# A hybrid decoder layer on one core: the S5 projection of the last four tiles and the first mixer's units of tile 4 placed earlier, four low parts moved to VectorE

## The chip, the cores and the metric

The kernel runs on one core of one Trainium2 chip. The metric is the device time of one execution in microseconds (us); less is better. The names of the engines in the rows are: PE is TensorE (matmuls), PEld its weight loads, DVE is VectorE, ACT is ScalarE, POOL is GpSimd, SP is SyncE, which here only issues transfers.

## What is computed

One decoder layer on x (1024 rows of 1024), float32. The input projection feeds three mixers: A is sliding-window attention with sinks, B is an S5 state-space layer, C is sparse attention with three branches. The three outputs are normalised each by itself, set side by side, and projected together. A feed-forward part follows.

```python
h = rms_norm(x, norm1_g[l]) * (1 + sc1) + sh1
aq, ak, av, su, cq, ck, cv, cg = jnp.split(h @ w_in[l], offsets, axis=-1)
o_a = swa_sink_mixer(aq, ak, av, a_q_gain[l], a_k_gain[l], a_sinks[l])   # 384 columns
o_b = s5_mixer(su, ...)                                                  # 256 columns
o_c = nsa_mixer(cq, ck, cv, cg, ...)                                     # 384 columns
mix = jnp.concatenate([rms_norm(o_a, g_a), rms_norm(o_b, g_b), rms_norm(o_c, g_c)], axis=-1)
x = x + ga1 * (mix @ w_out[l])
h = rms_norm(x, norm2_g[l]) * (1 + sc2) + sh2
x = x + ga2 * (jnp.square(jax.nn.relu(h @ w_ff1[l])) @ w_ff2[l])
```

## The kernel before

**Tiles and parts.** The 1024 rows are eight tiles (0 to 7) of 128 rows. A float32 product is made of three matmuls (`mm3`): both operands are split into a high part (`copy_hi`, a copy on ScalarE to the type fp32r) and a low part (`split_lo`, the subtraction of the high part, on VectorE or GpSimd), and high by high, high by low and low by high are added up in PSUM. The output projection of one tile has eight row blocks of `w_out` ("f"): 0 to 2 belong to mixer A, 3 and 4 to mixer B (S5), 5 to 7 to mixer C, and two halves of 512 columns. So mixer B's share of one tile is 2 halves x 2 blocks x 3 = 12 matmuls of 128x512.

**Stages.** First comes the input projection with the mixers' constants. Mixer A's units of tiles 0 to 3 run beside it (`a_phase`). Then `c_phase` runs mixer C's units of tiles 0 to 3, and beside it `early_ab` projects mixers A and B of tiles 0 to 3 and then loads the blocks 5 to 7. After each of these tiles `tile_end` normalises mixer C's output, projects it, adds the residual (`residual`), and forms the second norm and its transposed high and low parts (`norm2_steps`). With tile 4 the mixed stretch begins: the mixers' units of tiles 4 to 7 (A and C) are laid out in time T one after another, and `feed_forward` gives PE the feed-forward products of the first half (tiles 0 to 3) in between; it may start when tile 3's second norm is done ("N2 3"). When all units are done, `late_proj` loads the blocks of `w_out` again and projects tiles 4 to 7, mixer A's share first, then B's, then C's, adds the residual and forms the second norm; feed-forward products of the first half stand in between. The rest is the feed-forward part of the second half.

**What sets the order.** The program is written by generators and by steps put at planned times (`put`, `at`, `spawn`); `run_plan` records the calls in the order of the planned times, and `arrange` then lists them once more: each engine takes, of the recorded calls that are ready by its own costs, the first in recorded order. The result is a fixed order per engine, in which each engine issues its instructions one after another. SBUF pages have a tag and a number of slots (`SLOTS`: 38 of tag "b"), PSUM banks are given in rotation by `take`. All instructions are issued from one line (L2191), so the rows below are told apart by tile names and shapes: pa and pb are PSUM banks, b and u are pages, k holds keys, wide holds the unit matrix with which PE transposes.

**What the change touches.** `add_y` (line 1516) adds a projected half to the tile's page `y`; the first contribution is written with a factor per row, mixer B's has none (r is None). `early_ab` (1771) ends with "WO". `late_proj` (1806) goes through the groups of blocks:

```python
late, tiles, groups = {}, range(4, NT), ((0, 1, 2), (3, 4), (5, 6, 7), ())
...
if i == 1:
    late[n] = load_b(n)
    continue
```

`c_phase` (1864) lays out the units. At tile 4 the first unit of mixer A gets a stretch of its own, in which PSUM banks are dealt out anew (`mix_banks`), and `feed_forward` follows:

```python
if n == 4 and not kv and m == "a":
    s0, T = T, T + dur
    put(s0 - 3.5, mix_banks)
    spawn(s0 + X_T, feed_forward(), "N2 3")
    soft_end = T - C_GAP
```

`load_ff` (1905) loads a block of feed-forward weights and makes its high part on ScalarE and its low part on GpSimd (`split_lo(G, ...)`).

Of the kernel before, what the change touches and what calls it, by code (L numbers as in the profile page):

```python
# [9 lines left out]
F32 = mybir.dt.float32  # L10
# [3 lines left out]
ALU = mybir.AluOpType  # L14
# [6 lines left out]
NT = 8  # L21
# [289 lines left out]
def trunk(ctx: ExitStack, tc: tile.TileContext, I, out):  # L311
# [76 lines left out]
    def put(t, what):  # L388
        made_steps[0] += 1
        heapq.heappush(heap, (t, made_steps[0], what))  # L390
# [1125 lines left out]
    def add_y(n, c, o, r):  # L1516
        if n not in y:
            y[n] = page(1024)
            fresh[n] = set()
        d = y[n][:, c]  # L1520
        if c.start not in fresh[n]:
            fresh[n].add(c.start)
            ts(d, o, r, ALU.mult)
        elif r is None:
            tt(d, o, d, ALU.add)
        else:
            stt(d, o, r, d, ALU.mult, ALU.add)
# [204 lines left out]

    oA_d = dr.tile([NT, 128, 384], F32, name="oA_d")
    oC_d = dr.tile([4, 128, 384], F32, name="oC_d")

    def a_phase():

# [33 lines left out]
    def early_ab():  # L1771

        for f in range(5):
            load_wo(f)
            yield P_WO
        for n in range(NT // 2):
            while f"a {n}" not in done or "s5" not in done:
                yield 1.0
            o = load_o(oA_d[n])
            mb = load_b(n)  # L1780
            st = []
            steps = finish_steps(st, n * 2, lambda: o, 64, "b") + proj_steps(n, [0, 1, 2], st) + proj_steps(n, [3, 4], mb)
            for f in steps:
                f()
                yield P_TILE / len(steps)
        for f in range(5, 8):
            load_wo(f)
            yield P_WO
        load_row(2)
        done.add("WO")  # L1790

    def tile_end(n):

# [11 lines left out]

    def late_proj():

        late, tiles, groups = {}, range(4, NT), ((0, 1, 2), (3, 4), (5, 6, 7), ())
        for f in groups[0]:
            load_wo(f)  # L1810
            yield L_PACE
        for i, fs in enumerate(groups[:3]):
            for n in tiles:
                yield L_PACE
                if i == 1:
                    late[n] = load_b(n)
                    continue
                o, late[n] = load_o(oC_d[n - 4] if i else oA_d[n]), []
                for step in finish_steps(late[n], n * 2 + (16 if i else 0), lambda: o, 64 + fs[0]):
                    step()  # L1820
                    yield L_PACE
            for n in tiles:
                for dh in range(2):
                    c, o = slice(dh * 512, dh * 512 + 512), take("f2")
                    for j, f in enumerate(fs):
                        mm3(o, *late[n][0](j), WO[f][0][:, c], WO[f][1][:, c], j == 0, j == len(fs) - 1)
                    add_y(n, c, o, late[n][1])
                    yield L_PACE * len(fs)
                if 0 < n - 3 <= len(groups[i + 1]):
                    load_wo(groups[i + 1][n - 4])  # L1830
# [33 lines left out]
    def c_phase():  # L1864
# [10 lines left out]
        for n in range(NT):  # L1875
            units = [("a", kv, 0) for kv in range(2)] if n >= 4 else []
            units += [("c", kv, br) for kv in range(2) for br in (1, 2)]
            for m, kv, br in units:
                if m == "a":
                    dur = X_A  # L1880
                else:
                    np_ = (n + 1 if br == 1 else min(n + 1, 5)) + ((br == 2) == (n == NT - 1))
                    dur = np_ * (C_PART if n < 4 else X_PART) + C_FIX
                s0 = max(soft_end, T - dur * C_LEAD - C_GAP)
                soft_end = T - C_GAP
                if n == 4 and not kv and m == "a":
                    s0, T = T, T + dur
                    put(s0 - 3.5, mix_banks)
                    spawn(s0 + X_T, feed_forward(), "N2 3")
                    soft_end = T - C_GAP  # L1890
                unit_steps(m, n, kv, br, T, s0, soft_end, dur, Q)
                T += dur
                if n >= 4 and kv and br != 1:
# [11 lines left out]
    def load_ff(unit):  # L1905
# [2 lines left out]
        raw, hi, lo = page(1024), page(1024), page(1024)  # L1908
        nc.sync.dma_start(out=raw, in_=I["ff1"][i] if kind == 1 else I["ff2"][i, dh])
        copy_hi(hi, raw)  # L1910
        split_lo(G, lo, raw, hi)
        w_of[unit] = hi, lo

    def ff_act(o):
# [341 lines left out]
```

## Time and profile before

| | us |
|---|---|
| median of three executions | 1365.98 |
| lowest, highest | 1362.07, 1370.18 |
| the profiled execution | 1368.67 |
| its span, first to last instruction | 1367.0 |

The span lies 1.7 us under the time of the same execution. Busy times of the profile say how long an engine had an instruction; the ends of matmuls are modelled, so PE's busy time is an upper measure. PEclk is the granted clock of TensorE as a share of 2.4 GHz. "Idle before" names what ended the wait of an engine.

### The profile page before, as it was taken

Reading aid. Unit: us, or ns where it says so; the run is one execution under the profiler, and the core shown is the slowest. Engines: PE = TensorE matmul, PEld = TensorE weight load, DVE = VectorE, ACT = ScalarE, POOL = GpSimd, SP = SyncE. Lnnn points to the kernel's source line nnn. Section 1 sums busy time; section 2 is a strip of 40 time slices with the busy share of each in tenths; the row PEclk is TensorE's granted clock in tenths of the full one; section 3 lists DMA queues with packets and bytes.
Section 4 is the critical chain, followed back from the end, with each engine's and each line's share of the span. In section 5 each row is a group of like instructions: output and inputs, shape, how many; then the busy total and the mean of one; then the engine's idle time right before and its main releaser. Section 6 shows DMA issues by size and latency. Waiting matters only on the chain.

```text
span 1367.0 us, 19734 instructions
## 1 busy us (share of the span) xinstructions
PE 1306.1 (96%) x6862; PEld 1115.3 (82%) x6862; DVE 954.8 (70%) x1979; ACT 749.3 (55%) x1657; POOL 639.1 (47%) x604
## 2 busy tenths in 40 slices
PE   5998998998999869999999999999999999999998
PEld 4898998997787558888888888888787888888886
DVE  7868977787788545465565576463558887788896
ACT  6445367567666775565565565542354445544450
POOL 3477734034567365455465465575553233122230
PEclk9999999999899789999999999999999999999999
DMA  9445436223122222212222343244464432323221
GB/s 364 177 141 170 153 117 214 95 72 116 39 76 108 89 89 69 74 64 68 95 80 62 119 144 120 75 143 146 153 223 162 155 123 78 107 94 108 78 93 62
DMA packets 59570, 161.03 MB, mean 118 GB/s; under 512 B 6447, under 2 KB 22349, under 8 KB 59469
## 3 DMA queue, kind: packets, MB, share of 16 engines
q1 hardware_dynamic: 51661, 145.86, 32.3%
q10 hardware_dynamic: 7808, 13.91, 2.7%
q8 instruction: 54, 0.88, 0.3%
q14 instruction: 47, 0.39, 0.1%
HBM read 140.59 MB, written 19.14 MB: 117 GB/s over the span
## 4 chain that ended last, share of the span: by engine, by line
PE 76%; DVE 7%; ACT 3%; issue 2%; POOL 1%; DMA 1%; ACTq 0%; DVEq 0%; SPq 0%; POOLq 0%
PE pb L2191 41%; PE pa L2191 35%; DVE b L2191 4%; ACT b L2191 2%; DVE pb L2191 1%; ACT u L2191 1%; POOL b L2191 1%; DMA mixB_d<-b 1%; DVE k L2191 1%; DVE small L2191 0%; DVE u L2191 0%; DVE s L2191 0%; DMA b<-in_ada_dram 0%; ACT s L2191 0%; ACT k L2191 0%
## 5 line engine op out<-in xcount | busy, mean ns | idle before, releaser
L2191 PE MATMUL pb<-b,b 128*128 128x512 f32 (+2 forms) x2478 | 590.2, 385 | 1.4 <-DVE b L2191 1.3
L2191 PEld LDWEIGHTS pb<-b,b 128*128 128x128 f32 (+1 forms) x2478 | 446.0, 190 | 85.7 <-DVE b L2191 2.8
L2191 POOL TENSOR_TENSOR b<-b,b 128x1024 fp32r<-128x1024 f32 (+6 forms) x140 | 322.7, 2312 | 293.2 <-ACT b L2191 188.0
L2191 PE MATMUL pa<-b,b 128*128 128x512 f32 (+2 forms) x1830 | 364.3, 349 | 9.5 <-ACT b L2191 4.4
L2191 PEld LDWEIGHTS pa<-b,b 128*128 128x128 f32 (+1 forms) x1830 | 291.7, 195 | 49.8 <-ACT b L2191 5.3
L2191 ACT ACTIVATE b<-b 128x1024 fp32r<-128x1024 f32 (+4 forms) x266 | 242.0, 927 | 100.8 <-DMA b<-in_ff_dram 42.6
L2191 DVE TENSOR_TENSOR b<-b,b 128x1024 fp32r<-128x1024 f32 (+4 forms) x181 | 200.2, 1136 | 21.8 <-ACT b L2191 12.1
L2191 PE MATMUL pa<-u,b 128*128 128x384 f32 (+2 forms) x836 | 202.0, 364 | 7.4 <-DVE small L2191 2.0
L2191 PEld LDWEIGHTS pa<-u,b 128*128 128x128 f32 x836 | 148.3, 206 | 16.2 <-ACT u L2191 4.6
L2191 DVE TENSOR_TENSOR b<-pa,b 128x512 f32<-128x512 f32 (+2 forms) x168 | 107.6, 650 | 65.3 <-PE pa L2191 61.8
L2191 ACT ACTIVATE u<-pa 128x384 fp32r<-128x384 f32 (+4 forms) x205 | 97.1, 478 | 84.3 <-PE pa L2191 83.3
L2191 DVE TENSOR_TENSOR u<-pa,u 128x384 fp32r<-128x384 f32 (+1 forms) x173 | 94.9, 553 | 55.7 <-ACT u L2191 55.2
L2191 DVE TENSOR_TENSOR b<-pb,b 128x512 f32<-128x512 f32 (+2 forms) x120 | 76.2, 647 | 60.1 <-PE pb L2191 55.2
L2191 POOL TENSOR_SCALAR b<-b,small 128x64 f32<-128x64 f32 (+8 forms) x118 | 75.2, 648 | 68.9 <-DVE small L2191 55.8
L2191 PE MATMUL pa<-wide,b 128*128 128x128 f32 (+1 forms) x443 | 81.7, 296 | 24.8 <-DVE b L2191 19.1
L2191 POOL TENSOR_SCALAR u<-u,small 128x256 f32<-128x256 f32 (+3 forms) x90 | 55.1, 623 | 100.0 <-DVE small L2191 78.4
L2191 PEld LDWEIGHTS pa<-wide,b 128*128 128x128 f32 (+1 forms) x443 | 58.4, 149 | 43.5 <-DVE b L2191 21.2
L2191 POOL TENSOR_TENSOR b<-r,b 128x512 fp32r<-128x512 f32 x37 | 51.2, 1383 | 80.6 <-ACT b L2191 80.1
L2191 ACT ACTIVATE b<-pb 128x512 f32<-128x512 f32 (+3 forms) x60 | 29.1, 509 | 87.0 <-PE pb L2191 72.4
L2191 ACT ACTIVATE u<-pb,small 128x256 f32<-128x256 f32 (+6 forms) x126 | 60.2, 485 | 28.7 <-DVE small L2191 28.0
L2191 ACT ACTIVATE b<-pb,small 128x64 f32<-128x64 f32 (+4 forms) x130 | 62.5, 493 | 20.4 <-DVE small L2191 15.6
L2191 PE MATMUL pb<-k,u 128*128 128x320 f32 (+10 forms) x300 | 70.0, 344 | 2.3 <-ACT b L2191 2.1
(145 smaller groups left out, 1446.2 us busy)
## 6 DMA issues: line engine op xcount, KB each, us to landing
b<-in_ff_dram SPq DMA_DIRECT2D x128, 512.0 KB, 3.6
b<-in_ada_dram SPq DMA_DIRECT2D x48, 512.0 KB, 6.0
b<-in_x_dram SPq DMA_DIRECT2D x16, 512.0 KB, 7.1
b<-in_wo_dram SPq DMA_DIRECT2D x16, 512.0 KB, 4.3
r<-in_w_in_dram SPq DMA_DIRECT2D x16, 256.0 KB, 2.6
b<-in_cw_dram SPq DMA_DIRECT2D x8, 512.0 KB, 5.4
x_d<-b ACTq DMA_DIRECT2D x8, 512.0 KB, 3.2
out_dram<-b SPq DMA_DIRECT2D x16, 256.0 KB, 2.2
```

What stands on the lines that cost most here:

```text
L2191: method(*args, **kw)
```

## The change

It has three parts. Mixer B's share of the output projection of tiles 4 to 7 is made at the end of `early_ab`: four times `load_b`, 12 matmuls, two copies from PSUM to a page `y`, and a store of the page to a new buffer `yB_d` in DRAM; `late_proj` loads these pages back, no longer loads blocks 3 and 4 again, and adds only A's and C's share. The two units of mixer A of tile 4 are planned like those of tiles 0 to 3 (a shorter duration, a lead before the last unit of tile 3 ends), and the banks are dealt out anew at the first unit of mixer C of tile 4. The low parts of the first four feed-forward blocks go to VectorE.

```diff
@@ add_y
         if c.start not in fresh[n]:
             fresh[n].add(c.start)
-            ts(d, o, r, ALU.mult)
+            if r is None:
+                V.tensor_copy(out=d, in_=o)
+            else:
+                ts(d, o, r, ALU.mult)
@@ trunk
     oC_d = dr.tile([4, 128, 384], F32, name="oC_d")
+    yB_d = dr.tile([4, 128, 1024], F32, name="yB_d")
@@ early_ab
         load_row(2)
         done.add("WO")
+        for n in range(NT // 2, NT):
+            steps = proj_steps(n, [3, 4], load_b(n))
+            for f in steps:
+                f()
+                yield 6.0 / len(steps)
+            nc.scalar.dma_start(out=yB_d[n - 4], in_=y.pop(n))
@@ late_proj
-        late, tiles, groups = {}, range(4, NT), ((0, 1, 2), (3, 4), (5, 6, 7), ())
+        late, tiles, groups = {}, range(4, NT), ((0, 1, 2), (5, 6, 7), ())
...
-        for i, fs in enumerate(groups[:3]):
+        for i, fs in enumerate(groups[:2]):
             for n in tiles:
                 yield L_PACE
-                if i == 1:
-                    late[n] = load_b(n)
-                    continue
+                if not i:
+                    y[n] = page(1024)
+                    nc.sync.dma_start(out=y[n], in_=yB_d[n - 4])
@@ c_phase
                 if m == "a":
-                    dur = X_A
+                    dur = X_A if n > 4 else A_DUR
...
                 if n == 4 and not kv and m == "a":
-                    s0, T = T, T + dur
-                    put(s0 - 3.5, mix_banks)
-                    spawn(s0 + X_T, feed_forward(), "N2 3")
-                    soft_end = T - C_GAP
+                    s0 = max(soft_end, T - A_LEAD - A_GAP)
+                    spawn(T + 12.0, feed_forward(), "N2 3")
+                if n == 4 and not kv and m == "c" and br == 1:
+                    put(s0 + 0.0, mix_banks)
@@ load_ff
-        split_lo(G, lo, raw, hi)
+        split_lo(V if not half and kind == 1 and i < 4 else G, lo, raw, hi)
```

Since `arrange` lists everything anew, the order changes on all engines from the end of tile 2 on. Three places follow. In the change the issuing line is L2201.

On PE, between the output projection of tile 3 (its last matmul reads b_687) and the first feed-forward product (out pb_69, the last row). wide,b_693 are the transposes of tile 3's normed rows, wide,u_691 those of a unit of mixer A of tile 4. Before:

```order
L2191 MATMUL pa_65<-b_629,b_687 128x512
L2191 MATMUL pb_67<-b_395,u_689 128x256 x4
L2191 MATMUL pb_68<-b_395,u_689 128x256 x2
L2191 MATMUL pa_64<-wide,b_693 128x128
L2191 MATMUL pa_65<-wide,b_693 128x128
L2191 MATMUL pa_64<-wide,b_693 128x128
L2191 MATMUL pa_65<-wide,b_693 128x128
L2191 MATMUL pa_64<-wide,u_691 128x128 x3
L2191 MATMUL pa_65<-wide,q_692 128x128 x3
L2191 MATMUL pb_69<-b_652,b_700 128x512
```

In the change the transposes of tile 3's normed rows read b_712 (last row); ahead of them, behind the projection of tile 3, stand now the last half of tile 7's S5 projection (its last matmul is the first row), products of mixer A's unit of tile 4 with its values (pa_66) and scores of mixer C of tile 4 (k_444):

```order
L2201 MATMUL pa_64<-b_504,u_705 128x512
L2201 MATMUL pa_66<-u_710,b_358 128x384 x2
L2201 MATMUL pb_67<-k_444,u_702 128x352 x2
L2201 MATMUL pb_68<-k_444,u_702 128x352 x2
L2201 MATMUL pa_64<-wide,u_708 128x128 x3
L2201 MATMUL pa_66<-u_715,b_357 128x384
L2201 MATMUL pb_68<-k_444,u_702 128x352 x2
L2201 MATMUL pa_64<-wide,u_708 128x128 x3
L2201 MATMUL pa_66<-u_715,b_357 128x384
L2201 MATMUL pb_67<-k_444,u_702 128x352 x2
L2201 MATMUL pa_66<-u_717,b_358 128x384 x2
L2201 MATMUL pa_65<-wide,b_712 128x128
```

Before, only six score matmuls of mixer A (b_395) stood there.

On ACT, the end of mixer C's unit of tile 3 up to the high part of its normalised output, which the projection of tile 3 reads (b_687). Before:

```order
L2191 ACTIVATE u_683<-pa_64 128x384
L2191 ACTIVATE u_684<-pa_65,small 128x384
L2191 ACTIVATE s_686<-pa_66 64x384
L2191 ACTIVATE s_688<-s_645 128x384
L2191 ACTIVATE small<-small 128x1 x2
L2191 ACTIVATE b_703<-b_702 128x1024
L2191 ACTIVATE b_687<-s_645 128x384
```

In the change (there the high part is b_700, s_699 is the end of the unit, u_708 are exponentials of the second unit of mixer A of tile 4, yB_d the store of tile 6's page):

```order
L2201 DMA yB_d<-b_692 128x1024
L2201 ACTIVATE s_699<-pa_66 64x384
L2201 ACTIVATE u_702<-pa_63,small 128x384
L2201 ACTIVATE u_708,small<-pb_67,small 128x256
L2201 ACTIVATE s_701<-s_649 128x384
L2201 ACTIVATE u_708,small<-pb_67,small 128x256
L2201 ACTIVATE u_708,small<-pb_68,small 128x256
L2201 ACTIVATE small<-small 128x1 x2
L2201 ACTIVATE b_700<-s_649 128x384
```

Exponentials of tile 4 and a store stand now where a feed-forward block's high part (b_703) stood.

On SP's queue, the loads around the blocks 5 to 7 of `w_out` in `late_proj`. Before (the three last rows are these blocks):

```order
L2191 DMA u_1204<-oC_d 128x384
L2191 DMA b_1189<-in_ff_dram 128x1024
L2191 DMA u_1207<-oC_d 128x384
L2191 DMA u_1213<-oC_d 128x384
L2191 DMA b_1192<-in_wo_dram 128x1024
L2191 DMA b_1195<-in_wo_dram 128x1024
L2191 DMA b_1198<-in_wo_dram 128x1024
```

In the change (b_1159 is block 2, b_1178 and b_1181 are blocks 5 and 6):

```order
L2201 DMA u_1195<-oC_d 128x384
L2201 DMA b_1159<-in_wo_dram 128x1024
L2201 DMA b_1162<-yB_d 128x1024
L2201 DMA b_1166<-yB_d 128x1024
L2201 DMA b_1170<-yB_d 128x1024
L2201 DMA b_1174<-yB_d 128x1024
L2201 DMA u_1198<-oC_d 128x384
L2201 DMA b_1178<-in_wo_dram 128x1024
L2201 DMA b_1181<-in_wo_dram 128x1024
```

Four loads of stored pages stand ahead of the blocks 5 to 7.

## Rows read from the trace of the kernel before

**Rows 1.** The page: span, and busy times by engine.
```profile
span 1367.0 us, 19734 instructions
PE 1306.1 (96%) x6862; PEld 1115.3 (82%) x6862; DVE 954.8 (70%) x1979; ACT 749.3 (55%) x1657; POOL 639.1 (47%) x604
```

**Rows 2.** Busy times by stretch: length, each engine's us (x instructions), PEclk, DMA share, GB/s.
```profile
405.00:432.00 27.00, 25.75 (x147) 21.39 (x145) 21.31 (x72) 17.59 (x51) 18.84 (x19) 1.00 0.34 113
432.00:444.00 12.00, 11.19 (x58) 8.72 (x58) 11.53 (x39) 10.34 (x34) 11.33 (x13) 1.00 0.37 132
444.00:452.00 8.00, 5.96 (x24) 3.09 (x22) 5.15 (x13) 7.97 (x24) 4.81 (x6) 0.88 0.39 134
452.00:460.00 8.00, 6.68 (x25) 5.10 (x25) 4.36 (x10) 6.62 (x17) 0.01 (x1) 0.50 0.19 66
460.00:472.00 12.00, 9.11 (x49) 6.30 (x47) 7.32 (x17) 8.34 (x18) 3.92 (x4) 0.93 0.06 16
480.00:489.00 9.00, 0.00 (x0) 0.00 (x0) 3.25 (x10) 5.18 (x13) 7.20 (x8) 0.73 0.34 136
505.00:900.00 395.00, 394.71 (x2003) 329.78 (x2002) 233.48 (x623) 232.70 (x556) 218.06 (x168) 1.00 0.28 90
```

**Rows 3.** Who waited for whom, PE: us in total, times, longest us.
```profile
PE pa L2191 <- DVE b L2191: 21.4, 9, 9.5
```

**Rows 4.** Timeline of PE from tile 3's output projection on: start, us, what.
```profile
472.18 6.80 PE L2191 MATMUL pa<-b,b 128*128 128x512 f32 x18 [0.54 <-ACT b L2191]
...
489.21 0.69 PE L2191 MATMUL pa<-wide,b 128*128 128x128 f32 x2 [9.52 <-DVE b L2191]
...
492.52 1.20 PE L2191 MATMUL pb<-b,b 128*128 128x512 f32 x2
```

**Rows 5.** The chain of waits in that gap: start, us, engine.
```profile
483.81 2.52 POOL b L2191
...
486.87 0.19 POOL small L2191
```

**Rows 6.** The chain in the late feed-forward part, then the timeline of PE at 515.
```profile
1030.13 27.20 PE pb L2191 x120
...
515.38 0.49 PE L2191 MATMUL pa<-wide,u 128*128 128x128 f32 x3
515.62 0.60 PE L2191 MATMUL pa<-u,b 128*128 128x384 f32 x2
516.07 2.90 PE L2191 MATMUL pb<-b,b 128*128 128x512 f32 x12
```

**Rows 7.** Instructions by form of ACT and DVE: count, busy us, mean ns, idle before.
```profile
L2191 ACT ACTIVATE u<-pb,small 128x256 f32<-128x256 f32 x6 | 2.8, 470 | 0.2 <-DVE small L2191 0.2
L2191 ACT ACTIVATE u<-s 128x256 fp32r<-128x256 f32 x3 | 1.2, 405 | 0.0
L2191 ACT ACTIVATE b<-b 128x1024 fp32r<-128x1024 f32 x11 | 11.5, 1056 | 0.0
...
L2191 DVE COPY b<-pa 128x512 f32<-128x512 f32 x4 | 2.8, 691 | 2.5 <-PE pa L2191 2.5
L2191 DVE CUSTOM_DVE_ANT_1 pb<-pb,u,small 128x256 f32<-128x256 f32 x6 | 2.7, 489 | 0.0
```

**Rows 8.** Timeline in the late projection: a POOL subtraction and two equal ones of DVE.
```profile
912.05 2.40 POOL L2191 TENSOR_TENSOR b<-b,b 128x1024 fp32r<-128x1024 f32 x1
...
912.11 2.62 DVE L2191 TENSOR_TENSOR u<-s,u 128x256 fp32r<-128x256 f32 x1
...
915.25 0.45 DVE L2191 TENSOR_TENSOR u<-s,u 128x256 fp32r<-128x256 f32 x1
```

**Rows 9.** The first late product of PE, SP's loads of blocks 5 to 7; landing (page).
```profile
908.99 2.34 PE L2191 MATMUL pa<-b,u 128*128 128x512 f32 x9
...
925.31 5.89 SPq L2191 DMA_DIRECT2D b<-in_wo_dram  x3
...
b<-in_wo_dram SPq DMA_DIRECT2D x16, 512.0 KB, 4.3
```

## The prediction

> **What bounds the kernel now.** I read the page's busy times first: PE works for 1306.1 of 1367.0 us, no other engine for more than 70% [rows 1]. So time can only be gained where PE idles, or by giving it less to do where it doesn't. The stretches tell the two apart: from 505 to 900 PE is busy for 394.71 of 395.00 us, while between 444 and 472 it has 5.96, 6.68 and 9.11 of 8, 8 and 12 us, and between 480 and 489 nothing at all [rows 2]. The list of who waited for whom names the largest wait there: PE waits 9.5 us for a page "b" of DVE [rows 3]. On PE's timeline it lies between the projection of tile 3, which ends at 472.18 + 6.80 = 478.98, and the transposes of tile 3's normed rows at 489.21; the first feed-forward product comes at 492.52, 13.5 us after the projection [rows 4]. The chain of waits shows a POOL low part of 2.52 us at 483.81, ahead of the small POOL instruction of the norm at 486.87 [rows 5]. So one transition of some 50 us is loose; what follows it is tight.
>
> The sum is made against the profiled execution, 1368.67 us (span 1367.0), which lies 2.7 above the median of 1365.98; that much is taken off at the end. A measurement here can tell about 0.5%, 6.8 us, from no change.
>
> **The change part by part.** PE's products are the same ones at other places, so each term is work moved out of a tight stretch, or into a loose one.
>
> (a) *48 products leave the tight late part.* Four tiles times 12 products of 128x512. In the tight part such a product takes 27.20/120 = 0.227 us [rows 6]: 48 x 0.227 = **-10.9**. The bounds are equal to it within 0.1, as nothing idles there.
>
> (b) *Tile 4's units have run partly before the first feed-forward product.* By PE's order this is 10 transposes, 8 products 128x384 with the values and 16 score products. The timeline gives 0.24 us for three transposes (515.38 to 515.62), so 0.08 each, and 0.45 for two products with values (515.62 to 516.07), so 0.225 each [rows 6]; a score product is put at 0.19, by its width against the 384 columns. 0.8 + 1.8 + 3.0 = **-5.6**; they leave a part in which PE is full.
>
> (c) *The transition gets longer.* The first of the eight groups of six S5 products lands between 405 and 432, where PE has 25.75 of 27 us: 6 x 0.227 = 1.4 on the path. The other seven, and tile 4's units, fall into 444 to 472. PE has 28 - 21.75 = 6.25 us free there, and its half clock besides. But ACT gets six exponentials (0.470), four copies (0.405) and some nine more of that size, less two copies of a feed-forward block (1.056), about 2.8 + 1.6 + 4.0 - 2.1 = 6.3 us; DVE gets seven copies from PSUM (0.691) and eleven masks or subtractions (0.489), 4.8 + 5.4 = 10.2 us, short readouts not counted [rows 7]. In 444 to 472 ACT is busy for 22.93 of 28 us, DVE for 16.83 [rows 2]. Nothing shows that this dependent work can be packed to 100%. I take the density of the stretch just before, 432 to 444, in which ACT has 10.34 of 12 (0.862), DVE 11.53 (0.961), PE 11.19 (0.93) [rows 2]. ACT then needs (22.93 + 6.3)/0.862 = 33.9 us, 5.9 more than the 28; DVE (16.83 + 10.2)/0.961 = 28.1, 0.1 more; PE (21.75 + 9.5 of seven groups - 4.0 of clock)/0.93 = 29.3, 1.3 more. ACT decides: 1.4 + 5.9 = **+7.3**. Ends: 1.4 if all of it fits between, 1.4 + 6.3 + 10.2 = 17.9 if every added instruction of both engines is in the chain.
>
> (d) *The clock.* The granted clock is 0.88 from 444, when PE idles a quarter of the time, 0.50 (1.2 GHz) from 452 to 460, 0.93 after [rows 2]. Tile 3's 18 products take 6.80 us [rows 4], though 18 x 0.227 = 4.1 at full clock. With PE filled before it, I expect most of the 2.7 back: **-2.0**, ends 0 and -2.7.
>
> (e) *The norm of tile 3.* On DVE there now stand between the projection's last addition and the norm's scaling also a copy (0.69), two masks (2 x 0.489), two subtractions of an attention unit (2 x 0.45) and a low part of 128x1024, put at four times the 0.45 of a 128x256 one [rows 7, 8]: 0.7 + 1.0 + 0.9 + 1.8 = 4.4. DVE issues in order, so all that stands behind them waits. Against this goes the POOL low part of 2.52 ahead of the norm's small instruction [rows 5]. **+1.9**; ends -2.5 and +4.4. The 9 us of idle PE are filled by tile 4's units, which is term (b); the gap doesn't vanish, it holds work.
>
> (f) *The late projection's loads.* Two loads of `w_out` (and their high and low parts) and eight DVE additions go; four of stored pages come, ahead of the blocks 5 to 7 on SP's queue, and the four stores on ACT's queue, of which ACT only issues the start. Before, 44.4 us lie between the first product of mixer A (908.99) and the first of mixer C (953.40); in PE's new order 112 products, 112 x 0.227 = 25.4 us. SP issues block 5 at 925.31, 16.3 us after the first product, and two more 2.9 apart; a load lands in 4.3 [rows 9], then come ACT's copy, 1.056 [rows 7], and the low part, 2.40 [rows 8], 7.8 in all. At the old offset block 5 is there at 24.1, in time for 25.4; block 7 at 16.3 + 5.9 + 7.8 = 30.0, needed six products (1.4) later than 25.4, so 3.2 too late. The pages come free earlier too, as mixer B's part is gone, so I take half: **+1.6**. Ends: 0, and 7.8 + 2 x 2.9 = 13.6 if all is exposed.
>
> (g) *Low parts to VectorE.* What stays of them on the path is in (e); one POOL product then has no such neighbour ahead of it. That more is lost by both engines working at once is a rival below.
>
> Sum: -10.9 - 5.6 + 7.3 - 2.0 + 1.9 + 1.6 = -7.7, so 1368.67 - 7.7 = 1361.0 for the profiled execution and **1358.3** for the median.
>
> **The rivals.** *R1, no room in the transition.* The added ACT and DVE work is chained (exponentials, sums, scaling, transposes, copies alternate between the engines), and (c) is 17.9 rather than 7.3: -7.7 + 10.6 = +2.9, 1368.9. For it: around 452 PE, DVE and ACT all have holes at once, a sign of a chain, not of a full engine. Against: the new work belongs to other units than the chain, so it can go into the holes. Chance 0.18.
>
> *R2, all of it fits.* (c) costs 1.4, (d) gives 2.7, (e) gives 2.5, (f) is 0: -10.9 - 5.6 + 1.4 - 2.7 - 2.5 = -20.3, 1345.7. For it: 5.1 us of ACT and 11.2 of DVE idle in 444 to 472 against 6.3 and 10.2 added. Chance 0.19.
>
> *R3, the late weights come too late (slower).* If the stored pages ahead of them on SP's queue, or pages not yet free, hold back block 5 until all 13.6 us of load, copy and low part stand exposed, and the clock falls after that hole as it does at 452, where 8 us run at 0.50 (4.0 of work lost): -7.7 + 13.6 - 1.6 + 4.0 = +8.3, 1374.3. It begins to cost when block 5 is issued later than 25.4 - 7.8 = 17.6 us after the first late product. For it: SP issues in order, and the old offset is 16.3, only 1.3 away. Against: products of the feed-forward part stand ready in the pages and the order mixes them in. Chance 0.10.
>
> *R4, DVE and POOL in each other's way.* At 912 a DVE subtraction of 128x256 takes 2.62 us while a POOL one of 2.40 runs, an equal one 0.45 when none does [rows 8]: 2.2 lost. If three of the four moved low parts, or the norm's additions beside POOL's masks, meet that, 3 x 2.2 = 6.6: -1.1, 1364.9. Against: of wide two-operand POOL work only the factor on tile 3's rows remains at that place. Chance 0.08. The Trainium skill, "SBUF — State Buffer", section "Who interferes with whom", speaks against moving work to VectorE for this reason: the pair of ports that VectorE and GpSimd share is an exclusive lock, and an instruction of one that needs it holds up the other fully. By that rule, the trace agrees: 2.62 against 0.45.
>
> That the change doesn't do what it says is excluded by the order of PE, ACT and SP, in which the moved instructions stand.
>
> **How the numbers follow.** The forecast's own case has 0.45, with 1353 to 1363 as its range; two thirds of it lie under 1365.98 - 6.8 = 1359.2. Faster by over 0.5%: 0.30 + R2's 0.19 = 0.49. Within 0.5%: 0.15 of the forecast, 0.15 of R1 and 0.07 of R4 = 0.37. Slower: R3's 0.10, 0.03 of R1, 0.01 of R4 = 0.14. The range 1346 to 1371 takes in R1, nearly all of R2 and R4; outside lie R3 and the tails of R1 and R2, under 0.2.
>
> **What would show it.** Right: between 444 and 480 the granted clock stays near 1 and PE is fuller; tile 3's 18 products take about 4.1; the wait on DVE's page shrinks below 3 us with tile 4's products inside the gap; the first feed-forward product comes near 492.5 + 7.3 - 2.0 + 1.9 = 499.7; the first late product 5.6 us of work nearer to it than before, and mixer C's follow 25 to 29 us after mixer A's. (c) is wrong if the first feed-forward product comes before 494 (R2) or after 508 (R1); (f) if PE waits over 4 us for a page of `w_out` in the late projection (R3); (g) if the moved low parts take over 3 us on DVE (R4). The forecast as a whole is wrong if 505 to 900 is no longer full on PE, since (a) and (b) rest on that.

## The result, and the profile after

| | before | change |
|---|---|---|
| median of four executions each, us | 1368.08 | 1349.93 |
| lowest, highest | 1362.07, 1370.21 | 1347.43, 1350.46 |
| the profiled execution, us (span) | 1368.67 (1367.0) | 1350.46 (1348.7) |

The ratio is 0.9873, 95% interval 0.9844 to 0.9903: 18.2 us less, and the whole interval lies under 0.995, where the prediction begins to call a change faster. Two later series of the change against the kernel before gave 0.9861 [0.9842, 0.988] and 0.9896 [0.987, 0.9922]. The forecast of 1358.3 had the direction; the time lies inside its range of 1346 to 1371, but the gain was put at 7.7 us, and the time is under the 1353 to 1363 of the forecast's own case.

The page of the change (answers to [rows 1]); PE has the same 6862 products and is busy 10.9 us less, 1295.2 for 1306.1:

```profile
span 1348.7 us, 19750 instructions
PE 1295.2 (96%) x6862; PEld 1101.7 (82%) x6862; DVE 955.1 (71%) x1983; ACT 747.5 (55%) x1655; POOL 636.2 (47%) x598
```

Where the 18 us went is not seen by setting equal times side by side, since the change runs ahead early. PE's order is the same in both kernels for its first 2470 products, so the profiles are cut here at two events that both have: product 2400, the first of five transposes of width 128, and the first feed-forward product. On PE's timeline (start, us, what), product 2400 of before, then of the change:

```profile
401.14 0.71 PE L2191 MATMUL pa<-wide,b 128*128 128x128 f32 x5
```

```profile
393.81 0.71 PE L2201 MATMUL pa<-wide,b 128*128 128x128 f32 x5
```

And the busy times by stretch (length, us of each engine with its instructions in the order PE, PEld, DVE, ACT, POOL; granted clock; DMA share; GB/s), cut at these events. Before:

```profile
0.00:401.14 401.14, 366.94 (x2400) 341.34 (x2401) 310.29 (x754) 240.42 (x625) 194.15 (x286) 0.94 0.43 145
401.14:492.52 91.38, 72.73 (x355) 55.86 (x353) 59.90 (x170) 63.83 (x177) 55.44 (x57) 0.86 0.30 101
492.52:1367.00 874.48, 866.45 (x4111) 718.08 (x4109) 584.59 (x1057) 445.10 (x856) 389.55 (x262) 1.00 0.33 107
```

The change:

```profile
0.00:393.81 393.81, 356.75 (x2401) 330.67 (x2401) 308.14 (x754) 240.62 (x625) 193.97 (x286) 0.98 0.44 148
393.81:489.12 95.31, 86.17 (x437) 65.56 (x435) 75.22 (x215) 71.10 (x203) 51.15 (x58) 0.95 0.39 131
489.12:1348.70 859.58, 852.23 (x4029) 705.48 (x4027) 571.69 (x1017) 435.75 (x827) 391.12 (x255) 0.99 0.33 109
```

Three things are to be seen. The first stretch, in which no instruction of PE, DVE, ACT or POOL was moved, is 7.3 us shorter, at a mean granted clock of 0.98 instead of 0.94. The transition holds 82 more products and is only 3.9 us longer; PE is busy for 90% of it instead of 80%, and its clock is 0.95 instead of 0.86. The late stretch holds these 82 products less and is 14.9 us shorter. 14.9 - 3.9 = 11.0 us come from the moved work in this pair, 7.3 from the part in common.

Inside the transition of the change, PE's timeline:

```profile
471.47 0.63 PE L2201 MATMUL pa<-b,b 128*128 128x512 f32 x2
471.93 0.33 PE L2201 MATMUL pa<-u,b 128*128 128x384 f32 x1
472.33 3.94 PE L2201 MATMUL pa<-b,b 128*128 128x512 f32 x16
...
485.90 0.69 PE L2201 MATMUL pa<-wide,b 128*128 128x128 f32 x2 [1.04 <-DVE b L2201]
...
489.12 0.78 PE L2201 MATMUL pb<-b,b 128*128 128x512 f32 x1
```

Tile 3's 18 products (2 + 16) now take 476.27 - 471.47 = 4.80 us where [rows 4] had 6.80, the wait of 9.52 on DVE's page is 1.04, and from the end of the projection to the first feed-forward product it is 489.12 - 476.27 = 12.85 us, against 13.54. So the way to tile 3's projection is what grew: 471.47 - 393.81 = 77.66 us, against 472.18 - 401.14 = 71.04.

DVE and POOL in that place, on their timelines:

```profile
477.87 0.69 DVE L2201 COPY b<-pa 128x512 f32<-128x512 f32 x1 [0.69 <-PE pa L2201]
...
480.08 1.21 DVE L2201 TENSOR_TENSOR b<-b,b 128x1024 f32<-128x1024 f32 x1
...
481.75 1.21 DVE L2201 TENSOR_TENSOR b<-b,b 128x1024 fp32r<-128x1024 f32 x1
...
485.09 0.75 DVE L2201 TENSOR_SCALAR b<-b,small 128x1024 f32<-128x1024 f32 x1
```

```profile
477.56 2.39 POOL L2201 TENSOR_TENSOR b<-b,b 128x1024 f32<-128x1024 f32 x1
...
482.93 0.19 POOL L2201 TENSOR_SCALAR small<-small 128x1 f32<-128x1 f32 x1 [1.45 <-ACT b L2201]
```

The moved low part takes 1.21 us on DVE (481.75), behind the residual's sum (480.08) and while ACT makes the squares, so the norm's small instruction on POOL starts at 482.93, when ACT is done; before, a low part of 2.52 us stood ahead of it [rows 5].

### The profile page after: what moved, and what is told of

Same layout as the page of the kernel before. It is cut to its first block, busy times and chain, and to the rows that moved or that the text cites. A ratio compares the mean times of both kernels' runs of the same rounds, so it can differ in the third digit from the quotient of the medians.

```text
span 1348.7 us, 19750 instructions
## 1 busy us (share of the span) xinstructions
PE 1295.2 (96%) x6862; PEld 1101.7 (82%) x6862; DVE 955.1 (71%) x1983; ACT 747.5 (55%) x1655; POOL 636.2 (47%) x598
## 4 chain that ended last, share of the span: by engine, by line
PE 71%; DVE 9%; ACT 4%; DMA 3%; issue 2%; POOL 1%; ACTq 0%; SPq 0%; DVEq 0%; POOLq 0%
PE pb L2201 40%; PE pa L2201 32%; DVE b L2201 6%; ACT b L2201 2%; ACT u L2201 1%; DVE u L2201 1%; POOL b L2201 1%; DMA b<-in_ada_dram 1%; DVE pb L2201 1%; DMA mixB_d<-b 1%; DMA r<-in_w_in_dram 1%; DVE small L2201 0%; DVE k L2201 0%; DMA oC_d<-s 0%; ACT s L2201 0%
## 5 line engine op out<-in xcount | busy, mean ns | idle before, releaser
L2201 PE MATMUL pb<-b,b 128*128 128x512 f32 (+2 forms) x2466 | 586.8, 385 | 2.1 <-DVE b L2201 1.4
L2201 PEld LDWEIGHTS pb<-b,b 128*128 128x128 f32 (+1 forms) x2466 | 443.6, 190 | 87.5 <-DVE b L2201 3.3
L2201 POOL TENSOR_TENSOR b<-b,b 128x1024 fp32r<-128x1024 f32 (+6 forms) x134 | 315.9, 2365 | 266.5 <-ACT b L2201 186.7
L2201 PE MATMUL pa<-b,b 128*128 128x512 f32 (+2 forms) x1842 | 361.6, 345 | 8.7 <-ACT b L2201 4.2
L2201 PEld LDWEIGHTS pa<-b,b 128*128 128x128 f32 (+1 forms) x1842 | 289.1, 191 | 49.0 <-ACT b L2201 4.6
L2201 ACT ACTIVATE b<-b 128x1024 fp32r<-128x1024 f32 (+4 forms) x264 | 240.0, 925 | 110.3 <-DMA b<-in_ff_dram 32.4
L2201 DVE TENSOR_TENSOR b<-b,b 128x1024 fp32r<-128x1024 f32 (+4 forms) x185 | 202.2, 1124 | 16.5 <-ACT b L2201 7.4
L2201 PE MATMUL pa<-u,b 128*128 128x384 f32 (+2 forms) x836 | 197.8, 356 | 7.4 <-DVE small L2201 2.0
L2201 DVE TENSOR_TENSOR b<-pa,b 128x512 f32<-128x512 f32 (+2 forms) x165 | 105.4, 649 | 75.4 <-PE pa L2201 71.8
L2201 PEld LDWEIGHTS pa<-u,b 128*128 128x128 f32 x836 | 143.4, 200 | 17.5 <-ACT u L2201 4.8
L2201 ACT ACTIVATE u<-pa 128x384 fp32r<-128x384 f32 (+4 forms) x205 | 96.6, 478 | 84.3 <-PE pa L2201 81.0
L2201 DVE TENSOR_TENSOR u<-pa,u 128x384 fp32r<-128x384 f32 (+1 forms) x173 | 94.2, 552 | 48.0 <-ACT u L2201 47.4
L2201 POOL TENSOR_SCALAR u<-u,small 128x256 f32<-128x256 f32 (+3 forms) x90 | 59.0, 666 | 125.8 <-DVE small L2201 69.2
L2201 POOL TENSOR_SCALAR b<-b,small 128x64 f32<-128x64 f32 (+8 forms) x118 | 76.7, 661 | 74.8 <-DVE small L2201 60.2
L2201 DVE TENSOR_TENSOR b<-pb,b 128x512 f32<-128x512 f32 (+2 forms) x115 | 72.7, 644 | 52.9 <-PE pb L2201 47.9
L2201 PE MATMUL pa<-wide,b 128*128 128x128 f32 (+1 forms) x443 | 78.2, 287 | 16.0 <-DVE b L2201 11.1
L2201 POOL TENSOR_TENSOR b<-r,b 128x512 fp32r<-128x512 f32 x37 | 51.3, 1388 | 71.5 <-ACT b L2201 71.2
L2201 PEld LDWEIGHTS pa<-wide,b 128*128 128x128 f32 (+1 forms) x443 | 55.9, 144 | 34.2 <-DVE b L2201 12.9
L2201 ACT ACTIVATE b<-pb,small 128x64 f32<-128x64 f32 (+4 forms) x130 | 62.5, 493 | 28.1 <-DVE small L2201 16.6
L2201 ACT ACTIVATE u<-pb,small 128x256 f32<-128x256 f32 (+6 forms) x126 | 60.2, 484 | 27.5 <-DVE small L2201 25.0
L2201 PE MATMUL pb<-k,u 128*128 128x320 f32 (+10 forms) x300 | 70.5, 344 | 2.8 <-ACT b L2201 1.7
L2201 ACT ACTIVATE b<-pb 128x512 f32<-128x512 f32 (+3 forms) x60 | 28.9, 508 | 79.7 <-PE pb L2201 64.9
```

Of the source, the lines that this page charges most:

```text
L2201: method(*args, **kw)
```

## The experiments

All times below are in us. The columns come from the profile of each run: when product 2400 starts, from it to tile 3's projection, the length of the projection, from its end to the first feed-forward product ("ff"), from ff to the end; the last is the ratio of the times to those of before run beside it, with its 95% interval (it can differ by some 0.001 from the ratio of the medians).

| kernel | product 2400 at | to projection | projection | to ff | ff to end | 2400 to end | ratio |
|---|---|---|---|---|---|---|---|
| before | 401.1 | 71.0 | 6.8 | 13.5 | 874.4 | 965.8 | |
| before again | 402.6 | 71.0 | 6.8 | 13.6 | 874.6 | 966.0 | 1.000 [0.9977, 1.0023] |
| change | 393.8 | 77.7 | 4.8 | 12.9 | 859.5 | 954.9 | 0.9873 [0.9844, 0.9903] |
| change again | 401.5 | 77.4 | 4.8 | 12.9 | 854.4 | 949.5 | 0.9861 [0.9842, 0.988] |
| change, third | 394.0 | 76.6 | 4.8 | 12.9 | 857.0 | 951.3 | 0.9896 [0.987, 0.9922] |
| S5 early alone | 403.2 | 73.4 | 4.6 | 14.1 | 864.1 | 956.2 | 0.9931 [0.9911, 0.9951] |
| tile 4 early alone | 397.7 | 74.8 | 6.8 | 15.5 | 868.9 | 966.1 | 0.9992 [0.997, 1.0015] |
| low parts alone | 397.1 | 70.5 | 7.2 | 12.1 | 873.5 | 963.3 | 0.997 [0.9947, 0.9993] |
| S5 and tile 4 early | 399.6 | 76.6 | 4.8 | 13.8 | 856.9 | 952.0 | 0.9901 [0.9879, 0.9923] |
| S5 early, low parts | 402.4 | 73.4 | 4.5 | 11.2 | 863.4 | 952.5 | 0.9897 [0.9874, 0.992] |
| tile 4 and unread products | 401.7 | 77.3 | 10.0 | 16.6 | 868.6 | 972.4 | 1.0017 [0.9999, 1.0035] |
| slower pace, no low parts | 399.6 | 81.7 | 6.0 | 14.3 | 857.3 | 959.2 | 0.9915 [0.989, 0.994] |
| faster pace | 402.2 | 82.0 | 4.4 | 12.6 | 855.6 | 954.6 | 0.9928 [0.9902, 0.9954] |
| tile 4 six us later | 401.4 | 75.6 | 4.5 | 12.4 | 860.1 | 952.5 | 0.9894 [0.9871, 0.9917] |

**The kernel before, once more.** No edit.

> The kernel before once more, unchanged. PE's order is the same before and after the change up to its product 2470, which starts at 413.2 us in the profile of before and at 404.9 in that of after: 8.3 of the 18 us of difference lie ahead of the first moved instruction. Theory A (that is the granted clock of a single execution, not the change): this run's product 2470 starts elsewhere than 413.2, by several us, and the time differs accordingly; ratio 1.00 within its interval. Theory B (the changed program is faster in its common part too, by other addresses or other code): it starts at 413 within 1 us again.

Product 2400 at 402.6, ratio 1.000; from product 2400 on it agrees with the first profile within 0.2 us in every column. That is the yardstick for the table: what the profiles show from there on repeats well for this kernel. It doesn't hold for the change, whose three profiles lie between 949.5 and 954.9 from product 2400 on, so differences of up to 5 us between its variants are not told apart by one profile. The start moved by 1.5 us, which told the two theories apart badly; the runs below, with the same order up to there, did it.

**One part of the change at a time.** The three pieces of the diff above, each put into the kernel before by itself.

> The early S5 projection alone (units of tile 4 and low parts as before). Theory A, by the terms of the forecast: 48 x 0.227 = 10.9 us less in the late part, the first feed-forward product later by about 3 to 6 us (seven groups of six products, seven copies of 0.69 us on DVE beside the units of tiles 2 and 3), about -5 to -8 in all: 0.994 to 0.996. Rival, all hidden: -11 or more, 0.992. Rival, in full on the chain: -3 or less, 0.998.

> The units of mixer A of tile 4 planned ahead alone. Theory A: work of 5.6 us of PE goes into the idle 9.5 us at tile 3's norm; the first feed-forward product stays within 2 us of 492.5 of the profile before (against the same start), and the end comes 4 to 6 us earlier: 0.996. Rival: the units' exponentials and masks hold up tile 3's own chain and give it back, 0 us, 1.000.

> The low parts of the first four feed-forward blocks on VectorE alone. Theory A: it takes POOL's 2.5 us from tile 3's norm, so the first feed-forward product comes 1 to 3 us earlier after product 2400 than in before (91.4 us there), and nothing else moves: 0.998 to 0.999. Rival (shared ports, or DVE's own queue before the norm): no gain or up to 3 us later, 1.000 to 1.002.

The S5 projection alone: the transition grows by 0.8 us and the late part shrinks by 10.3, so 9.6 from product 2400 on, 9.0 in the medians. That lies between Theory A (5 to 8) and the rival (11 or more), and Theory A's 3 to 6 us for the first feed-forward product were wrong. Its busy times by stretch, which the transition's row above of before (355 products, 91.38 us) is to be held against:

```profile
403.24:495.36 92.12, 78.24 (x403) 60.35 (x401) 67.04 (x181) 64.79 (x181) 51.52 (x56) 0.93 0.37 127
495.36:1359.50 864.14, 855.54 (x4063) 708.87 (x4061) 575.21 (x1046) 441.90 (x850) 395.64 (x262) 1.00 0.32 109
```

48 more products, 7.1 us more of DVE, 0.8 us longer: all but hidden, at a granted clock of 0.93 instead of 0.86. By the table the 0.8 is made of 2.4 more up to tile 3's projection, 2.2 less in it and 0.6 more behind it. Tile 4's units alone:

```profile
397.68:494.87 97.19, 81.64 (x395) 62.83 (x394) 68.22 (x209) 73.35 (x208) 60.95 (x65) 0.87 0.30 105
494.87:1363.70 868.83, 859.78 (x4070) 713.12 (x4068) 577.26 (x1017) 435.96 (x826) 397.16 (x255) 1.00 0.31 107
```

The transition grows by 5.8 us and the late part shrinks by 5.6: nothing is left, 0.9992 with an interval on both sides of 1. That is the rival named there; "within 2 us of 492.5" was wrong. ACT has 9.5 us more to do in it, and the wait before tile 3's transposes doesn't go away but is cut up by it. The low parts alone take 1.6 us from the transition (13.5 to 12.1 behind the projection) and 1.0 from the rest.

**Two parts together.**

> Both moves, the low parts on GpSimd as before. Theory A: the two moves add up; the low parts on VectorE are worth 0 to 2 us at tile 3's norm, so within 2 us of the change itself: 0.987 to 0.990. Rival: the low parts carry the norm (POOL's 2.5 us stands in front of it), so 4 us or more behind the change: over 0.990.

> The change without its middle part: early S5 projection and low parts on VectorE, the units of tile 4 as in before. By adding up the single runs (from product 2400 to the first feed-forward product 92.1 with the projection alone and 89.8 with the low parts alone, against 91.4; from there to the end 864.1 with the projection alone, against 874.4). Theory A (the parts add up): 90.5 and 863, so 953.5 from product 2400, within 4 us of the change's two profiles (954.9 and 949.5): the units of tile 4 give in the late part what they take in the transition; ratio 0.988 to 0.992. Rival (the units need both others to pay): over 957, ratio 0.993 or more.

S5 and tile 4 together: 952.0. S5 and the low parts together: 952.5, with 89.1 us of transition where Theory A expected 90.5. Both lie between the change's own profiles (949.5 to 954.9). So the sum over single parts is nearly the whole: in the transition +0.8 + 5.8 - 1.6 = +5.0 against +2.9 to +3.9 for the change, in the late part -10.3 - 5.6 - 1.0 = -16.9 against -14.9 to -20.0. Tile 4's units bring next to nothing on top of the other two by these profiles; the ratios of 0.9897 without them and 0.9861 to 0.9896 with them have intervals that overlap.

**Products that only fill PE.** Tile 4's units early, and at the end of `early_ab` products nobody reads:

```diff
+        for n in range(NT // 2, NT):
+            for dh in range(2):
+                c, o = slice(dh * 512, dh * 512 + 512), take("pj")
+                for i, f in enumerate([3, 4]):
+                    mm3(o, *mb[0](i), WO[f][0][:, c], WO[f][1][:, c], i == 0, i == 1)
+                yield 3.0
```

> Tile 4's units early, and beside them 48 products of 128x512 whose result nobody reads (hi and lo page of tile 3, the same blocks of w_out), at the places of the early S5 projection; the late projection as in before. Work is added, none taken away. Theory A (PE, filled in the transition, keeps its full clock, and that is what lets the units of tile 4 in for nothing): no half clock between 440 and 480, and from product 2400 to the first feed-forward product at most 95 us, against 97.2 with the units alone, although 10.9 us of products are added; ratio 0.998 to 1.000. Rival (the products cost their time, the gain of both together comes from other places): 99 us or more, ratio 1.002 or more.

The clock came as expected: in the same 36 us, 444 to 480, it is 0.95 here and 0.76 with the units alone (0.78 in the stretch that lies 4.0 us earlier, as their product 2400 does).

```profile
444.00:480.00 36.00, 31.61 (x159) 22.11 (x157) 22.87 (x64) 29.96 (x85) 11.56 (x17) 0.95 0.27 90
```

```profile
444.00:480.00 36.00, 30.13 (x126) 22.35 (x126) 20.05 (x57) 26.37 (x75) 13.16 (x17) 0.76 0.31 101
```

The time did not: 103.8 us of transition, 6.6 more than with the units alone. Theory A falls: the higher clock goes with 33 more products in these 36 us, but tile 3's chain waits for other engines. On PE's timeline its projection, 10.0 us long, stops for 1.86 us for a page of DVE, which has scores of tile 4 listed ahead of it; and on POOL's timeline a low part of 2.36 us, listed there as before, stands between the two small instructions of the norm:

```profile
483.81 5.07 PE L2197 MATMUL pa<-b,b 128*128 128x512 f32 x14 [1.86 <-DVE b L2197]
```

```profile
498.48 0.19 POOL L2197 TENSOR_SCALAR small<-small 128x1 f32<-128x1 f32 x1
498.75 2.36 POOL L2197 TENSOR_TENSOR b<-b,b 128x1024 fp32r<-128x1024 f32 x1
501.07 0.55 POOL L2197 TENSOR_TENSOR small<-small 128x1 f32<-128x1 f32 x1
```

Such a low part is what the change takes from POOL. So a filled PE at a higher clock did not by itself let the units in for nothing.

**Other places for the same work.** The change, or the change without its low parts, with one number altered: the pace of the early S5 projection (9 or 4 planned us a tile for 6), or six planned us added ahead of tile 4's units.

```diff
-                yield 6.0 / len(steps)
+                yield 9.0 / len(steps)
```

```diff
-                yield 6.0 / len(steps)
+                yield 4.0 / len(steps)
```

```diff
                 if n == 4 and not kv and m == "a":
+                    T += 6.0
```

> A try at a better version: the change with the low parts on GpSimd as before, and the early S5 projection spread over nine planned us a tile instead of six, so that its last groups stand among the work beside tile 3's norm. Theory A: the 4 us of idle PE there shrink to about 2 and the half clock behind it is shorter: 1 to 4 us less than the change, 0.986 to 0.989. Rival (the norm's chain on DVE, ACT and POOL sets the first feed-forward product, not PE): within 1 us of the variant with six, 0.990.

> The change with the early S5 projection at four planned us a tile instead of six: all its groups stand ahead of tile 3's projection, none behind it. Nine us a tile made the transition 6.9 us longer than six (102.0 against 95.1), by putting the last groups between tile 3's projection and its norm. Theory A (what delays tile 3's own chain is what costs): the transition takes 1 to 3 us less than the change's 95.1 to 95.3, the end part is the same 854 to 860. Rival (PE then stands idle at the norm again and loses what it won): 95 or more.

> The change with the units of tile 4 planned six us later, so that on PE the transposes of tile 3's normed rows stand ahead of part of tile 4's scores and products. Theory A (the units' instructions ahead of the norm cost the 3.7 to 5.8 us by which the transition grew): the first feed-forward product 2 to 4 us earlier after product 2400 (91 to 93), the end part up to 2 us longer, as less of tile 4 is done by then; in sum 1 to 3 us under the change. Rival: the order behind the norm only trades one for the other, within 1 us.

Both other paces are worse in the transition: 102.0 and 99.0 us against 94.3 to 95.3. Both come to tile 3's projection late, after 81.7 and 82.0 us against 76.6 to 77.7. In the slower one two S5 products stand besides among the projection, which takes 6.0 us; in the faster one all 48 stand ahead of it. Which of the instructions ahead hold it up was not taken apart. My theory for the slower one was wrong, its rival (within 1 us of the variant with six) too, and so was the theory for the faster one. Tile 4's units six us later did bring the first feed-forward product forward by 1.8 to 2.9 us and did cost the late part about as much (860.1 against 854.4 to 859.5): 952.5, a trade, as the rival there said. None of these beats the change.

**The change once more, twice.**

> The change itself once more. Theory A (of the 18 us shown first, some 8 were the clock of the part that both kernels have in common): over more executions the difference falls to about 11 us, ratio 0.990 to 0.993, and product 2400 of PE starts later than in the first profile of the change (393.8) in this one. Theory B (the common part is faster by the change): ratio 0.987 again, product 2400 near 394. From product 2400 to the first feed-forward product both expect the 95.3 us of the first profile, and from there to the end 859.6.

> The change a third time, for what is still open: from PE's product 2400 to the end its two profiles took 954.9 and 949.5 us, before 965.8 and 966.0, so the moved part is worth 11 or 16.5 us, while the medians differ by 18.4. Theory A (the moved part gives 11 to 16.5, the rest is the clock granted in the common part ahead of product 2400): this profile lies between 949 and 956 from product 2400 on, the medians differ by more than that part in most rounds, and of the executions those with the lower mean clock are the slower ones. Theory B (the moved part gives all 18): 948 or less from product 2400 on.

Its transition repeats (95.3, 95.1, 94.3); its late part varies with the granted clock and a few short waits (859.5, 854.4, 857.0); product 2400 starts at 393.8, 401.5 and 394.0. The second run refuted the size in its Theory A: the ratio stayed at 0.9861 although product 2400 was back at 401.5 in its profile. That start refutes its Theory B as well. In the third, Theory A held for the profile, 951.3 us from product 2400 on, 14.6 under before; the medians of that series differ by 1369.23 - 1353.9 = 15.3. Its six executions go by their mean clock: 1347.0 at 0.987, 1351.0 to 1354.5 at 0.984, 1355.9 and 1356.9 at 0.979 and 0.980.

## Why the prediction was right, and where it was short

The forecast's sum was -7.7 us. From product 2400 on, the three profiles of the change show -11.0, -16.4 and -14.6 against the mean of before's two (965.9), -14.0 in the mean. So the moved work gave 6.3 us more than forecast: 2.6 in (e), 2.6 in the late part and 1.1 in (c). That the time still lies in the range is due to the range being drawn wide enough for R1 and R2. By its terms:

- **(a) and (b), -10.9 and -5.6: right.** Alone, the S5 projection took 10.3 us from the late part, tile 4's units 5.6. The reason given, that a part in which PE is full gives back every product taken from it, holds: 866.45 of 874.48 us busy before, 855.54 of 864.14 with 48 products less. From 505 to 900 PE stays full in the change too, with 393.98 of 395.00 us.
- **(c), +7.3: right in size, by luck and not for its reason.** The way to tile 3's projection grew by 6.6, 6.4 and 5.6 us. But the working let ACT decide by its density, over the 28 us up to 472. In the whole transition of the change ACT is busy for 71.10 of 95.31 us, 75%, and DVE for 79%; neither is full. S5 alone took 2.4 us there and tile 4's units 3.8. That they cost this by standing in the lists ahead of tile 3's chain fits the runs with the same work at other places (82.0 us to the projection with all S5 products ahead, 75.6 with tile 4's units later), but no run shows which instruction it was.
- **(d), -2.0: right.** The 18 products went from 6.80 to 4.80. It is the S5 projection that brings it (4.6 alone); with tile 4's units alone they take 6.8 as before. The granted clock over the 18 is 0.62 before, 0.66 with tile 4's units alone, and 1.00 with S5 alone and in the change.
- **(e), +1.9: wrong, -0.7.** The step that failed is the one that added up all the instructions that DVE has between the projection's last addition and the scaling, and set against them the whole 2.52 us of POOL. On the timelines, the copy and DVE's next instructions, on scores of tile 4 and on an attention unit, run while POOL makes its product on tile 3's rows (477.56 to 479.95), and the low part, 1.21 us and not 1.8, while ACT makes the squares. What does cost is two more instructions on scores of tile 4, listed ahead of the scaling: it starts at 485.09, 1.3 us after POOL's second small instruction ends (483.76).

```profile
483.21 0.55 POOL L2201 TENSOR_TENSOR small<-small 128x1 f32<-128x1 f32 x1
...
484.03 0.47 DVE L2201 CUSTOM_DVE_ANT_0 pb<-pb,b 128x288 f32<-128x288 f32 x1
...
484.58 0.59 DVE L2201 CUSTOM_DVE_ANT_0 pb<-pb,b,small 128x352 f32<-128x352 f32 x1
```

Before, the squares were done at 485.72, so of POOL's 2.52 us (483.81 to 486.33) only the end was on the path: with another instruction of POOL behind it the small one came at 486.87 [rows 5], 1.15 us after the squares, in the change 0.1 us after them. The low parts alone gave 1.4 us back in this place.

```profile
485.52 0.20 ACT L2191 ACTIVATION_READ_ACCUMULATOR b<-b 128x1 f32 x1
...
486.31 0.47 POOL L2191 TENSOR_SCALAR u<-u,small 128x256 f32<-128x256 f32 x1
```

- **(f), +1.6: wrong, no cost is seen.** The late part is shorter by 14.9, 20.1 and 17.5 us in the three profiles; less the 16.5 of (a) and (b) this leaves +1.6, -3.6 and -1.0, which is too wide to tell a size. Of the 5.2 us between the first two, 3.7 are PE's busy time, at a granted clock of 0.99 in the first and 1.00 in the second. PE's idle time is the closer measure of loads that come late: 8.0 us before, 7.4 in the first profile of the change, 5.9 and 7.9 in the second and third, whose late parts are

```profile
496.53:1350.90 854.37, 848.49 (x4029) 703.55 (x4027) 572.07 (x1017) 435.11 (x827) 386.68 (x255) 1.00 0.32 109
```

```profile
488.28:1345.30 857.02, 849.14 (x4029) 703.37 (x4027) 573.94 (x1017) 435.40 (x827) 392.27 (x255) 1.00 0.32 109
```

The step that failed held SP to its old offset. Of the three loads that began 16.3 us behind the first late product [rows 9], two are now issued 8.6 us ahead of it and the third 9.0 behind it:

```profile
881.98 2.05 SPq L2201 DMA_DIRECT2D b<-yB_d  x4
...
887.72 0.81 SPq L2201 DMA_DIRECT2D b<-in_wo_dram  x2
...
905.31 0.33 SPq L2201 DMA_DIRECT2D b<-in_wo_dram  x1
```

```profile
896.27 2.33 PE L2201 MATMUL pa<-b,u 128*128 128x512 f32 x9
...
924.00 2.34 PE L2201 MATMUL pa<-b,u 128*128 128x512 f32 x9
```

Mixer C's products follow 27.7 us after mixer A's, as forecast (25 to 29), and the last of the three loads is issued 18.7 us ahead of them. Why SP comes to them earlier was not tested. Before, SP's longest waits between 905 and 932 us are for pages "u" of DVE (us in total, times, longest), to which the loads of oC_d ahead of block 5 go; in the change the third load comes after a wait for PE:

```profile
SPq L2191 <- DVE u L2191: 16.7, 3, 8.6
```

```profile
SPq L2201 <- PE pb L2201: 14.9, 1, 14.9
```

**The rivals.** R1 (no room, +2.9) is out: (c) cost 6.2 us in the mean and not 17.9. R2 (all fits, 1345.7) came nearest in time but not in mechanism, since (c) did cost its 6 us. By the prediction's own sign R2 would hold, as the first feed-forward product came at 489.12, before 494; but that sign goes by a start that moved. Counted from before's product 2400 it is 401.14 + 95.31 = 496.5, between 494 and the forecast's 499.7. R3 did not come, as the loads show. R4 did not come at tile 3's norm: the low part above took 1.21 us, and POOL's product on tile 3's rows was over at 477.56 + 2.39 = 479.95, before it began. Its meeting did come for the fourth of the moved low parts, but there POOL paid, which had begun second, with 3.32 us for a low part of 2.40 [rows 8]; all three profiles of the change show it (3.32, 3.34, 3.18). In the first of them PE goes on without a stop there. The Trainium skill, "SBUF — State Buffer", section "Who interferes with whom", says that a VectorE instruction with two SBUF inputs contends with a GpSimd instruction that reads SBUF; the trace agrees, with 3.32 us against 2.40:

```profile
497.31 1.22 DVE L2201 TENSOR_TENSOR b<-b,b 128x1024 fp32r<-128x1024 f32 x1
```

```profile
497.46 3.32 POOL L2201 TENSOR_TENSOR b<-b,b 128x1024 fp32r<-128x1024 f32 x1 [2.79 <-ACT b L2201]
```

**What is left.** 1368.08 - 1349.93 = 18.2, and 17.8 between the median of all fifteen executions of the change (1350.6) and that of before beside its own repeat (1368.4), against 14.0 from product 2400 on. Some 4 us thus belong to the part in which both kernels have the same order, or to the executions that happened to be profiled. Over all fourteen profiles of this study product 2400 starts between 393.8 and 403.2. The granted clock shows where a quick start comes from: there are places at which it falls in one execution of the same instructions and not in another. Two of them, 50 to 70 and 180 to 195 us, before, in the change, and in the change again:

```profile
50.00:70.00 20.00, 17.95 (x94) 15.74 (x93) 15.29 (x21) 7.77 (x10) 9.49 (x18) 0.83 0.41 158
180.00:195.00 15.00, 15.00 (x85) 14.50 (x84) 7.50 (x19) 7.77 (x17) 2.74 (x2) 0.77 0.33 103
```

```profile
50.00:70.00 20.00, 17.85 (x106) 15.25 (x106) 17.91 (x25) 10.38 (x13) 9.80 (x12) 1.00 0.52 199
180.00:195.00 15.00, 15.00 (x105) 14.75 (x104) 13.40 (x31) 10.81 (x22) 4.88 (x4) 1.00 0.38 122
```

```profile
50.00:70.00 20.00, 17.96 (x94) 15.67 (x93) 15.29 (x21) 7.79 (x10) 9.55 (x18) 0.83 0.42 158
180.00:195.00 15.00, 15.00 (x85) 14.49 (x84) 7.84 (x16) 7.69 (x17) 2.74 (x2) 0.77 0.33 108
```

The fall at the first place comes and goes between two executions of the change, so it isn't the change that takes it away; the run with the low parts alone, where PE has before's order up to its product 2704, also has 1.00 there. The second place is at 1.00 in two of the change's three profiles and in none of the other eleven (0.77 to 0.79). Whether the change makes the quick starts likelier, or fell on them, was not settled.

## What to carry to other kernels

Cut two profiles at events that both have, not at equal times: here 7 of 18 us lay in a part that the change doesn't touch. Work that is moved out of a saturated stretch was worth nearly its full duration (10.3 of 10.9 us) and could be priced from one row; what it costs where it goes was not told here by the free time of the engines there: what counts is whether it stands ahead of the chain that ends that stretch, as the two instructions ahead of the scaling did. And price the parts of a change one by one: tile 4's units looked like the reason for a filled gap and gave as much as they took.

## What the runs showed of the hardware

The same kernel took 1360.4 to 1374.3 us over its executions, and the mean granted clock of an execution goes with it: of the twelve executions of the kernel before, the quickest (1360.58) had 0.981 and the slowest (1373.74) 0.971. A difference of 0.5% between two single executions of this kernel is inside that. At the same place of the program (50 to 70 us) the granted clock was 0.83 in one execution of the change and 1.00 in another.

DVE's low part of 128x1024 took 1.21 us and POOL's 2.40 [rows 8], for the same operation and types: the moved ones are twice as quick, which is why moving them costs DVE less than it relieves POOL.

Where two such low parts overlapped in these runs, the one that began second took longer. POOL's took 3.32 us in the change, begun 0.15 us after DVE's, which kept its 1.22. In the run with tile 4 six us later DVE's, begun 0.65 us after POOL's, took 2.84:

```profile
500.83 2.41 POOL L2202 TENSOR_TENSOR b<-b,b 128x1024 fp32r<-128x1024 f32 x1 [1.18 <-ACT b L2202]
```

```profile
501.48 2.84 DVE L2202 TENSOR_TENSOR b<-b,b 128x1024 fp32r<-128x1024 f32 x1
```
